# A two-layer network on one core: smaller first loads, a bank of its own for 256 columns, another order of GLA's state matmuls, and weight rows at shifted offsets

## Chip, cores and metric

The kernel runs on one core of one Trainium2 chip. The metric is the device time of one execution in microseconds. TensorE (PE) multiplies, VectorE (DVE) and ScalarE (ACT) work on tiles beside it, GpSimd (POOL) and SyncE (SP) do little but start transfers.

## What is computed

256 tokens of width 1024 pass two blocks and a last norm, all in float32.

```python
def first_block(x, mem, ...):
    h = rms_norm(x, norm_mix); z = h @ w_in
    z_rnn, z_q, z_k, z_v, z_g, z_dec, z_mq, z_gate = split(z)
    out_a = rg_lru(causal_dwconv(z_rnn))
    out_b = rms_norm(chunked_gla(z_q, z_k, z_v, log_alpha)) * silu(z_g)
    mk, mv = split(rms_norm(mem, mem_norm) @ w_mem_kv)
    out_c = softmax(z_mq @ mk.T) @ mv
    merged = sum(sigmoid(z_gate) * (branches @ w_branch))
    x = x + merged @ w_out
    gate_h, val_h = split(causal_dwconv(rms_norm(x) @ w_up))
    x = x + (gelu(gate_h) * val_h) @ w_down
    return rms_norm(x, final_norm)

# chunked_gla, per chunk of 64 tokens and per head:
    state = d_n[..., None] * state + einsum("bhjd,bhjv->bhdv", k_n, v_n)
```

The second block has attention with 6 heads, an SSD scan and a pooling mixer beside each other, then a SwiGLU FFN of width 2816 and the final norm, whose result is the output (256 x 1024).

## The kernel before

**Weights.** The kernel streams all weights once, in chunks of mostly 1024 x 256 (1 MB). A chunk is loaded by one DMA on SP's queue into one of three `raw` tiles and treated in two halves of four k rows (a k row: 128 partitions by 256 columns). Each half is split in two numbers, `wh` by a copy to the matmul's reduced type on ACT (L156) and `wl`, the rest, by a subtraction on DVE (L157); `emit_half` (L169 on) does both, three halves ahead of use (`AHEAD`), into five buffers each. The activations are kept split in the same way.

**Matmuls.** `mm3` (L202 to 205) makes one product from three matmuls: high by high, high by low, low by high. `chunk_T` holds the weights stationary and moves the 256 tokens, `chunk_tok` holds 128 tokens and moves 256 weight columns; both collect in one PSUM bank from the pool `psp`, of four, while everything else uses the four banks of `aup` (`aux`). `PLACE` puts both halves of the chunks up3, xbc3 and gu6 at an offset of 28 and 30 elements in their tiles; all other halves begin at 0.

**Order.** The chunks run in the order of `wplan`: memory keys and values (memk, memv), mq, zrnn, qk, the two gates of the recurrence, v, g, then for each of three branches four gate chunks alternating with four branch chunks (gate2_0, br2_0, ... gate0_0, br0_0, ... gate1_0, ...), wout, the first FFN (up and dn), the second block's input chunks (vz, qk2, xbc, pool), wo2, and the second FFN (gu and dn2_). Smaller pieces of work, as attention or GLA, are generators in two `lanes`; `step()` advances each by one `yield` between two chunks, and a tile scheduler fixes the order on each engine.

**GLA's state.** `gla_state` (L707 to 732) makes, for chunks 0, 1 and 2 of 64 tokens, k transposed times v for four heads. Chunk n stands on partitions 64 (n mod 2) on. Per chunk four matmuls of 64 rows (L720) fill two banks; ACT copies chunk 0, DVE adds the decayed state before for the others; then it yields. `gla_out` follows in the lane.

**Start.** The first two chunks, memk0 and memk1, are interleaved and come in pieces of two k rows: 128x512 of `memT` (the memory, transposed), then 128x512 of each chunk, four times, all on SP's queue; 16 columns of parameters (`par`, among them the norm gain that scales `memT`) come on ACT's queue. ACT scales and rounds memT (L159), DVE makes the rest (L160). Thirteen matmuls of ones (L258) run ahead of the first product. Sums of squares of memT are made with ACT (L282), DVE and two matmuls (L297).

**Second FFN and final norm.** `accs_tok` starts four banks with x3 transposed, two per tile of 128 tokens, of 512 columns each; `down_tok` adds every dn2_ chunk to them and `last_tok` the last ones, tile 0 first. Then, for each tile, ACT squares both banks (L1337) with a sum over columns, DVE adds the two sums (L1341, L1342), ACT takes the root (L1343), and four DVE instructions make the reciprocal and one Newton step (L1344 to 1347). For tile 1, the product of the first 512 columns with the gain `nfb` is made early, ACT scales it (L1354) and starts its DMA; DVE scales the other 512 in two pieces (L1331), each with a DMA on SP (L1360).

Of the kernel before, what the change touches and what calls it, by code (L numbers as in the profile page):

```python
# [9 lines left out]
F32 = mybir.dt.float32  # L10
# [63 lines left out]
for _n in ("up3", "xbc3", "gu6"):  # L74
    PLACE[_n, 0] = 28
    PLACE[_n, 1] = 30

# [38 lines left out]
def build(ctx: ExitStack, tc: tile.TileContext, ins: dict, out: bass.AP):  # L116
# [52 lines left out]
    def emit_half(parts=1, between=None):  # L169
# [12 lines left out]
        m = n // 2  # L182
        e = PLACE.get((name, i), 0)
# [47 lines left out]
    def chunk_tok(name, x, nk=KT, wide=False, k_outer=False):  # L231
# [3 lines left out]
        for i in range(2):  # L235
# [3 lines left out]
            if k_outer:  # L239
                od.sort(key=lambda q: q[1])  # L240
# [11 lines left out]
    par = cp.tile([P, NPAR], F32, name="par")  # L252
    nc.scalar.dma_start(par[:, :16], ins["par"][:, :16])
# [3 lines left out]
    for _ in range(13):  # L257
        pe.matmul(wps, ones, ones, start=True, stop=True)  # L258
    memr = slot("R1", [P, KT, S])
# [3 lines left out]
    def pv(name, i=0, n=1, rows=P):  # L263
        o, c = POFF[name]
        return par[:rows, o + i:o + i + n]
# [77 lines left out]
    def mem_part(i):  # L343
        nc.sync.dma_start(memr[:, 2 * i:2 * i + 2, :], ins["memT"][:, 2 * i:2 * i + 2, :])
        for k in (2 * i, 2 * i + 1):
            split(mh[:, k, :], ml[:, k, :], memr[:, k, :], pv("g_mem", k))


    first = ("memk0", "memk1")
    fps = [bank(), bank()]  # L350
    fw = {}
    for q in range(4):
        mem_part(q)
        for n, name in enumerate(first):
            if q == 0:
                raws[name] = wrp.tile([P, WMAX], F32, tag="raw", name=uid("raw"))
# [3 lines left out]
            o = WOFF[name][0]  # L360
            cr = slice(512 * q, 512 * q + 512)
            c = slice(512 * (q % 2), 512 * (q % 2) + 512)
            nc.sync.dma_start(raws[name][:, cr],
                              W[o:o + P * 2048].rearrange("(p n) -> p n", p=P)[:, cr])
            split(fw[n][0][:, c], fw[n][1][:, c], raws[name][:, cr])
            for k in range(2):
                for mo in range(2):
                    w0 = c.start + k * 256 + mo * P
                    kk = 2 * q + k
                    mm3(fps[n][:, mo, :], fw[n][0][:, w0:w0 + P], fw[n][1][:, w0:w0 + P],  # L370
                        mh[:, kk, :], ml[:, kk, :], kk == 0 and mo == 0, kk == KT - 1, skip=True)
# [13 lines left out]
    nc.sync.dma_start(par[:, 16:], ins["par"][:, 16:])  # L385
# [321 lines left out]
    def gla_state():  # L707
# [6 lines left out]
        for n in range(3):  # L714
            r = slice(64 * (n % 2), 64 * (n % 2) + 64)
            for hp in range(2):
                ps = aux([P, 2, DV])
                for i in range(2):
                    hd = 2 * hp + i
                    pe.matmul(ps[:DK, i, :], kt[r, n // 2, hd * DK:(hd + 1) * DK],  # L720
                              gv[r, n // 2, hd * DV:(hd + 1) * DV], start=True, stop=True)
                if n == 0:
                    act.activation(sts[0][:, hp * 384:(hp + 1) * 384],
                                   ps[:DK].rearrange("p a b -> p (a b)"), AF.Copy)
                else:
# [591 lines left out]
    def last_tok(ws, phs, accs):  # L1317
        act.activation(warm, last_u[0][:, 0, 0:1], AF.Sqrt, scale=0.0, bias=ones[:, 0:1])
        for t in range(2):
            c = slice(t * P, (t + 1) * P)  # L1320
            for n in range(2):
                q = slice(n * 512, (n + 1) * 512)
                for k, ((wh, wl), (ph, pl)) in enumerate(zip(ws, phs)):
                    mm3(accs[2 * t + n], ph[:, c], pl[:, c], wh[:, 0, q], wl[:, 0, q],
# [5 lines left out]
    def scaled(dst, acc, r, nf):  # L1330
        dve.scalar_tensor_tensor(dst, acc, r, nf, op0=ALU.mult, op1=ALU.mult)  # L1331

    for t in range(2):
        ssq = small([P, 2])
        o = [t2(), t2()]
        for n in range(2):
            act.activation(t2(), accs[2 * t + n], AF.Square, accum_out=ssq[:, n:n + 1])  # L1337
            if t == 1 and n == 0:
                dve.tensor_tensor(o[0], accs[2], nfb[:, 0:512], op=ALU.mult)
        v, r, q = small([P, 1]), small([P, 1]), small([P, 1])  # L1340
        dve.tensor_scalar(v, ssq[:, 0:1], 1.0 / D, EPS, op0=ALU.mult, op1=ALU.add)  # L1341
        dve.scalar_tensor_tensor(v, ssq[:, 1:2], 1.0 / D, v, op0=ALU.mult, op1=ALU.add)  # L1342
        act.activation(r, v, AF.Sqrt)  # L1343
        dve.reciprocal(r, r)  # L1344
        dve.tensor_tensor(q, r, r, op=ALU.mult)
        dve.scalar_tensor_tensor(q, q, -0.5, v, op0=ALU.mult, op1=ALU.mult)
        dve.scalar_tensor_tensor(r, q, 1.5, r, op0=ALU.add, op1=ALU.mult)
        rows = slice(t * P, (t + 1) * P)
        if t == 0:
            for n in range(2):  # L1350
                scaled(o[n], accs[n], r, nfb[:, n * 512:(n + 1) * 512])
                nc.sync.dma_start(out[rows, n * 512:(n + 1) * 512], o[n])
        else:
# [141 lines left out]
```

## Time and profile before

| | |
|---|---|
| runs | 796.61, 797.58, 798.03 us; median 797.58 us |
| profiled execution | 797.59 us |
| its span | 795.8 us |
| PE busy | 785.1 us (99%), 6460 records |
| DVE busy | 598.6 us (75%) |
| ACT busy | 481.8 us (61%) |
| DMA | 144.03 MB, mean 181 GB/s |
| granted TensorE clock, mean | 0.998 |

The span is what the profiler sees of the program; the profiled execution took 1.8 us more than it. Times in rows are counted from the span's start. A row of a timeline has the start, the duration of the instruction or the group (x count), the engine, the line, the operation with output and inputs, and in brackets the idle time ahead of it and what ended it. Matmuls overlap, so the starts of two neighbours tell their spacing, not their durations.

### The profile page before, as it was taken

How to read it: one execution, taken by the hardware profiler on the slowest of the kernel's cores; microseconds unless marked ns; L12 is line 12 of the kernel's file. 1: busy time of each engine (PE TensorE's matmuls, PEld its weight loads, DVE VectorE, ACT ScalarE, POOL GpSimd, SP SyncE). 2: the span in 40 equal slices, each digit the busy share in tenths (PEclk: the TensorE clock that was granted, in tenths of full speed). 3: DMA queues.
4: the chain of work that ended last, by engine and by line, in shares of the span. 5: the costliest groups of instructions: out<-in, count | busy, mean ns of one | idle time of the engine just before them, and what ended most of it. 6: DMA issues, size and time to landing. Idle time of an engine off the chain costs nothing.

```text
span 795.8 us, 15612 instructions
## 1 busy us (share of the span) xinstructions
PE 785.1 (99%) x6460; PEld 760.9 (96%) x6460; DVE 598.6 (75%) x980; ACT 481.8 (61%) x770; POOL 10.2 (1%) x23
## 2 busy tenths in 40 slices
PE   8999999999999999999999999999999999999996
PEld 8999989999889999999999999999899999999995
DVE  6988757965667777898778887899898756656663
ACT  6845679964345555666556565768976544444443
POOL 0000110000000000000000000000000000000000
PEclk9999999999999999999999999999999999999999
DMA  8864544364445665366555555263174544555521
GB/s 281 305 229 152 175 133 176 114 231 140 144 142 201 203 213 204 110 243 228 171 203 207 173 204 198 103 257 113 49 268 157 215 181 167 203 200 180 205 106 53
DMA packets 23526, 144.03 MB, mean 181 GB/s; under 512 B 2896, under 2 KB 3424, under 8 KB 8480
## 3 DMA queue, kind: packets, MB, share of 16 engines
q1 hardware_dynamic: 22464, 140.98, 49.9%
q0 software_dynamic: 704, 1.80, 0.6%
q8 instruction: 50, 0.82, 0.4%
q10 hardware_dynamic: 288, 0.27, 0.1%
q14 instruction: 20, 0.16, 0.1%
HBM read 141.20 MB, written 1.05 MB: 179 GB/s over the span
## 4 chain that ended last, share of the span: by engine, by line
PE 91%; DVE 4%; ACT 3%; issue 1%; DMA 1%; DVEq 0%; SPq 0%; ACTq 0%
PE ps L203 23%; PE ps L204 22%; PE ps L205 22%; PE aux L203 6%; PE aux L205 6%; PE aux L204 5%; DVE wl L157 2%; PE aux L521 1%; PE ps L220 1%; PE ps L227 1%; PE ps L218 1%; DMA raw<-w 1%; ACT wh L156 1%; PE aux L720 1%; ACT L1154 0%
## 5 line engine op out<-in xcount | busy, mean ns | idle before, releaser
L157 DVE TENSOR_TENSOR wl<-raw,wh 128x1024 fp32r<-128x1024 f32 (+4 forms) x276 | 322.1, 1172 | 119.5 <-ACT wh L156 117.7
L156 ACT ACTIVATE wh<-raw 128x1024 fp32r<-128x1024 f32 (+4 forms) x276 | 277.9, 1015 | 207.2 <-PE ps L204 159.6
L203 PE MATMUL ps<-H,wh 128*128 128x256 f32 x1320 | 368.2, 279 | 1.2 <-ACT wh L156 1.2
L205 PE MATMUL ps<-H,wl 128*128 128x256 f32 x1320 | 366.3, 278 | 0.2 <-DVE wl L157 0.2
L204 PE MATMUL ps<-H,wh 128*128 128x256 f32 x1320 | 366.3, 278 | 0.0
L203 PEld LDWEIGHTS ps<-H,wh 128*128 128x128 f32 x1320 | 248.0, 188 | 3.5 <-issue 1.8
L204 PEld LDWEIGHTS ps<-H,wh 128*128 128x128 f32 x1320 | 248.7, 188 | 0.3
L205 PEld LDWEIGHTS ps<-H,wl 128*128 128x128 f32 x1320 | 248.1, 188 | 0.4 <-DVE wl L157 0.4
L203 PE MATMUL ps<-wh,H 128*128 128x256 f32 (+2 forms) x192 | 54.6, 285 | 0.0
L204 PE MATMUL ps<-wl,H 128*128 128x256 f32 (+2 forms) x192 | 54.0, 281 | 0.3 <-DVE wl L157 0.3
L205 PE MATMUL ps<-wh,H 128*128 128x256 f32 (+2 forms) x192 | 54.1, 282 | 0.0
L205 PE MATMUL aux<-S,wl 128*128 128x256 f32 x192 | 53.1, 277 | 0.0
L204 PE MATMUL aux<-S,wh 128*128 128x256 f32 x192 | 53.1, 276 | 0.0
L203 PE MATMUL aux<-S,wh 128*128 128x256 f32 x192 | 53.1, 276 | 0.0
L156 ACT ACTIVATE S<-t 128x256 fp32r<-128x256 f32 x46 | 19.0, 415 | 50.3 <-DVE t L921 26.5
L543 DVE SCALAR_TENSOR_TENSOR t<-t,par,t 128x255 f32<-128x255 f32 (+1 forms) x96 | 40.1, 478 | 0.1
L204 PEld LDWEIGHTS ps<-wl,H 128*128 128x128 f32 x192 | 36.1, 188 | 0.5 <-DVE wl L157 0.5
L203 PEld LDWEIGHTS ps<-wh,H 128*128 128x128 f32 x192 | 36.1, 188 | 0.4 <-issue 0.4
L205 PEld LDWEIGHTS ps<-wh,H 128*128 128x128 f32 x192 | 36.1, 188 | 0.0
L205 PEld LDWEIGHTS aux<-S,wl 128*128 128x128 f32 x192 | 36.1, 188 | 0.0
L203 PEld LDWEIGHTS aux<-S,wh 128*128 128x128 f32 x192 | 36.1, 188 | 0.0
L204 PEld LDWEIGHTS aux<-S,wh 128*128 128x128 f32 x192 | 36.1, 188 | 0.0
(327 smaller groups left out, 1070.8 us busy)
## 6 DMA issues: line engine op xcount, KB each, us to landing
raw<-w SPq DMA_DIRECT2D x115, 1024.0 KB, 4.8
raw<-w SPq DMA_DIRECT2D x12, 768.0 KB, 4.3
raw<-w SPq DMA_DIRECT2D x12, 256.0 KB, 5.3
raw<-w SPq DMA_DIRECT2D x2, 896.0 KB, 4.5
raw<-w SPq DMA_DIRECT2D x1, 1088.0 KB, 6.2
raw<-w SPq DMA_DIRECT2D x1, 1048.0 KB, 4.8
R<-memT SPq DMA_DIRECT2D x4, 256.0 KB, 5.5
R<-xT SPq DMA_DIRECT2D x2, 512.0 KB, 8.8
```

The source lines that it names most:

```text
L156: act.activation(dst_h, src, AF.Copy)
L157: dve.tensor_tensor(dst_l, src, dst_h.bitcast(F32), op=ALU.subtract)
L203: pe.matmul(o, lh, rh, start=start, stop=False, skip_group_check=skip)
L204: pe.matmul(o, lh, rl, start=False, stop=False, skip_group_check=skip)
L205: pe.matmul(o, ll, rh, start=False, stop=stop, skip_group_check=skip)
L218: pe.matmul(ps[:, m, :], wh[:, k, c], x[0][:, kk, :], start=kk == 0 and m == 0, stop=False, skip_group_check=True)
L220: pe.matmul(ps[:, m, :], wl[:, k, c], x[0][:, kk, :], start=False, stop=False, skip_group_check=True)
L227: pe.matmul(ps[:, m, :], wh[:, k, m * P:(m + 1) * P], x[1][:, kk, :], start=False, stop=kk == nk - 1, skip_group_check=True)
L521: pe.matmul(ps[r0:r1, :], mv[:, mt, hd * DV + d0:hd * DV + d0 + r1 - r0], pts[hd][:, mt, :], start=mt == 0, stop=mt == 1, skip_group_check ...
L543: dve.scalar_tensor_tensor(dst[:, s:], src[:, :S - s], w(width - 1 - s), dst[:, s:], op0=ALU.mult, op1=ALU.add)
L720: pe.matmul(ps[:DK, i, :], kt[r, n // 2, hd * DK:(hd + 1) * DK], gv[r, n // 2, hd * DV:(hd + 1) * DV], start=True, stop=True)
```

## The change

- **Shifted rows.** A table `LEAD` names 14 chunks. In the first half of each, the first k row (or the first two) lies at an offset of 28 and 30 (or 4 and 2) modulo 32 elements of its tile, the rest at 0 modulo 32; `Rows` hands out the rows. The half is split in two pieces, so with two instructions on ACT and two on DVE. Entries that end in `True` run the first half with k outermost. `PLACE` gets gu3.
- **First loads.** The 16 parameter columns come in front of memT in the same tensor, so that the first piece is 128x272 on SP; the first two k rows of memk0 come as two pieces of 128x256 on ACT's queue; k row by k row is split for memk0. Ten matmuls of ones for thirteen.
- **GLA's state.** Chunks 0 and 1 take turns matmul by matmul, into four banks, and there are two yields in place of three.
- **Second FFN.** The last 512 columns of token tile 1 lie in two banks, of which one is taken from the pool of four that the chunks rotate through; in `down_tok` the runs of 256 go ahead of those of 512.
- **Final norm.** Another form of the root's correction, with doubled gains; for tile 1 all products are made part by part; one DVE instruction and one DMA for the second 512 columns.

The diff, cut:

```diff
-for _n in ("up3", "xbc3", "gu6"):
+for _n in ("up3", "xbc3", "gu6", "gu3"):
     PLACE[_n, 0] = 28
     PLACE[_n, 1] = 30
+LEAD = {
+    "mq1": (28, 30, True),
+    "qk0": (28, 30, True),
+    "gate2_0": (28, 30, True),
+    "gate0_1": (28, 30, True),
+    "gate0_3": (28, 30, True),
+    "memv0": (4, 2, True),
+    "v2": (28, 30, False),
+    "zrnn2": (28, 30, False),
+    "gate2_2": (28, 30, False),
+    "gu2": (28, 30, False),
+    "gate2_3": (28, False),
+    "gate0_0": (30, False),
+    "gate2_1": (4, 2, True),
+    "pool": (4, 2, False),
+}
+class Rows:
+    def __init__(self, t, b, n, lead):
+        self.t, self.b, self.n = t, b, n
+        self.off, o = [], 0
+        for k in range(n):
+            r = lead[k] if k < len(lead) else 0
+            o += (r - o) % 32
+            self.off.append(o)
+            o += b
+    def __getitem__(self, i):
+        _, k, c = i
+        a, e, _ = c.indices(self.b)
+        return self.t[:, self.off[k] + a:self.off[k] + e]
+    def parts(self):
+        b, n, m = self.b, self.n, self.lead
+        d = self.off[m - 1] - self.off[0] if m == 2 else b
+        head = self.t[:, self.off[0]:self.off[0] + m * d].rearrange("p (a b) -> p a b", a=m)[:, :, :b]
+        rest = self.t[:, self.off[m]:self.off[m] + (n - m) * b].rearrange("p (a b) -> p a b", a=n - m)
+        return (head, slice(0, m * b), m), (rest, slice(m * b, n * b), n - m)
...
+        if i == 0 and name in LEAD:
+            hs, ls = (Rows(w, b, a // 2, LEAD[name][:-1]) for w in (wh, wl))
+            for (h, c, r), (l, _, _) in zip(hs.parts(), ls.parts()):
+                split(h, l, raw[:, c].rearrange("p (a b) -> p a b", a=r))
+            loaded[name, i] = (hs, ls)
+            return
...
-            if k_outer:
+            if k_outer or i == 0 and LEAD.get(name, (False,))[-1]:
                 od.sort(key=lambda q: q[1])
...
+    nc.sync.dma_start(memall[:, :272], ins["memT"][:, :272])
+    for k in range(2):
+        first_w(nc.scalar, "memk0", slice(256 * k, 256 * k + 256))
+    nc.sync.dma_start(memr[:, 1, :], ins["memT"][:, 272:528])
+    first_w(nc.sync, "memk1", slice(0, 512))
...
+                if q == 0 and n == 0:
+                    c = slice(256 * k, 256 * k + 256)
+                    split(mh[:, kk, :], ml[:, kk, :], memr[:, kk, :], pv("g_mem", kk))
+                    split(fw[n][0][:, c], fw[n][1][:, c], raws[name][:, c])
...
-        for n in range(3):
-            r = slice(64 * (n % 2), 64 * (n % 2) + 64)
+        for ns in ((0, 1), (2,)):
             for hp in range(2):
-                ps = aux([P, 2, DV])
+                pss = [aux([P, 2, DV]) for _ in ns]
                 for i in range(2):
                     hd = 2 * hp + i
+                    for n, ps in zip(ns, pss):
+                        r = slice(64 * (n % 2), 64 * (n % 2) + 64)
...
+        accs = [aux([P, 512]) for _ in range(4)] + [bank([P, 512])]
...
+    RUNS = (((0, 0, 512), (1, 512, 512)), ((2, 0, 512), (3, 512, 256), (4, 768, 256)))
...
-                for n in range(2):
-                    q = slice(n * 512, (n + 1) * 512)
-                    mm3(accs[2 * t + n], ph[0][:, k, c], ph[1][:, k, c], wh[:, 0, q], wl[:, 0, q],
+                for a, q0, nq in sorted(RUNS[t], key=lambda r: r[2]):
+                    q = slice(q0, q0 + nq)
+                    mm3(accs[a][:, :nq], ph[0][:, k, c], ph[1][:, k, c], wh[:, 0, q], wl[:, 0, q],
...
+    act.activation(nfb, nfb, AF.Copy, scale=2.0)
...
+        for i, (a, q0, nq) in enumerate(parts):
+            act.activation(t2()[:, :nq], a[:, :nq], AF.Square, accum_out=ssq[:, i:i + 1])
+            if early:
+                q = q0 % 512
+                dve.tensor_tensor(o[q0 // 512][:, q:q + nq], a[:, :nq], nfb[:, q0:q0 + nq], op=ALU.mult)
...
+        act.activation(root, ssq[:, n - 1:], AF.Sqrt, scale=1.0 / D, bias=v[:, n - 2:n - 1])
+        dve.scalar_tensor_tensor(v[:, n - 1:], ssq[:, n - 1:], 1.0 / D, v[:, n - 2:n - 1],
+                                 op0=ALU.mult, op1=ALU.add)
+        dve.reciprocal(u, root)
+        dve.scalar_tensor_tensor(u, v[:, n - 1:], u, root, op0=ALU.mult, op1=ALU.add)
+        dve.reciprocal(u, u)
...
```

On ACT, at the start of the program, the kernel before has these rows (H is memT scaled and rounded, R is memT as loaded, t holds squares):

```order
L253 DMA par<-par 128x16
L255 ACT_TABLE_LOAD
L255 ACTIVATE warm<-ones 128x1
L159 ACTIVATE H_3_105<-R_1_102,par 128x256 x2
L156 ACTIVATE wh_115<-raw_114 128x512
L282 ACTIVATE t_22_277<-R_1_102 128x512
L156 ACTIVATE wh_133<-raw_132 128x512
L159 ACTIVATE H_3_105<-R_1_102,par 128x256 x2
```

and the changed one these:

```order
L315 DMA raw_86<-w 128x256 x2
L323 ACT_TABLE_LOAD
L323 ACTIVATE warm<-ones 128x1
L206 ACTIVATE H_5_108<-R_1_85 128x256
L203 ACTIVATE wh_112<-raw_86 128x256
L206 ACTIVATE H_5_108<-R_1_85 128x256
L203 ACTIVATE wh_112<-raw_86 128x256
L203 ACTIVATE wh_134<-raw_87 128x512
L206 ACTIVATE H_5_108<-R_1_85 128x256 x2
```

The parameter load is gone from ACT's queue and two weight loads stand there; one k row of memT and 256 columns of memk0 are split at a time, and the first square has moved behind them.

On TensorE, in the lane of GLA, the first group of state matmuls of the kernel before stands between a branch chunk and a gate chunk (V holds k transposed, S holds v, aux are PSUM banks):

```order
L205 MATMUL ps_2175<-M_159_1286,wl_2115 128x256
L720 MATMUL aux_2226<-V_204_1543,S_271_2087 96x192 x2
L720 MATMUL aux_2230<-V_204_1543,S_271_2087 96x192 x2
L203 MATMUL ps_2234<-H_39_325,wh_2144 128x256
```

and in the changed kernel, at the same place:

```order
L258 MATMUL ps_2191<-M_159_1294,wl_2129 128x256
L792 MATMUL aux_2242<-V_204_1551,S_271_2101 96x192
L792 MATMUL aux_2243<-V_204_1551,S_271_2101 96x192
L792 MATMUL aux_2242<-V_204_1551,S_271_2101 96x192
L792 MATMUL aux_2243<-V_204_1551,S_271_2101 96x192
L792 MATMUL aux_2251<-V_204_1551,S_271_2101 96x192
L792 MATMUL aux_2252<-V_204_1551,S_271_2101 96x192
L792 MATMUL aux_2251<-V_204_1551,S_271_2101 96x192
L792 MATMUL aux_2252<-V_204_1551,S_271_2101 96x192
L256 MATMUL ps_2260<-H_39_327,wh_2158 128x256
```

The group now holds eight matmuls for chunks 0 and 1 in turn, in four banks; a second group of four, for chunk 2, stands where the second of three stood, and what follows in the lane stands one place earlier.

On DVE, at the end of the program, for token tile 1, before (aux are the banks of the result, GQ the gain, sm columns of one number):

```order
L1339 TENSOR_TENSOR t_1202_9471<-aux_8024,GQ_7605 128x512
L1341 TENSOR_SCALAR sm_9478<-sm_9470 128x1
L1342 SCALAR_TENSOR_TENSOR sm_9478<-sm_9470,sm_9478 128x1
L1344 RECIPROCAL sm_9479<-sm_9479 128x1
L1345 TENSOR_TENSOR sm_9480<-sm_9479 128x1
L1346 SCALAR_TENSOR_TENSOR sm_9480<-sm_9480,sm_9478 128x1
L1347 SCALAR_TENSOR_TENSOR sm_9479<-sm_9480,sm_9479 128x1
L1331 SCALAR_TENSOR_TENSOR t_1203_9472<-aux_8025,sm_9479,GQ_7605 128x256 x2
```

and in the changed kernel:

```order
L1422 TENSOR_TENSOR t_1206_9569<-aux_8052,GQ_7631 128x512
L1425 TENSOR_SCALAR sm_9566<-sm_9565 128x1
L1422 TENSOR_TENSOR t_1207_9570<-aux_8053,GQ_7631 128x256
L1427 SCALAR_TENSOR_TENSOR sm_9566<-sm_9565,sm_9566 128x1
L1422 TENSOR_TENSOR t_1207_9570<-ps_8054,GQ_7631 128x256
L1430 SCALAR_TENSOR_TENSOR sm_9566<-sm_9565,sm_9566 128x1
L1432 RECIPROCAL sm_9567<-sm_9568 128x1
L1433 SCALAR_TENSOR_TENSOR sm_9567<-sm_9566,sm_9567,sm_9568 128x1
L1434 RECIPROCAL sm_9567<-sm_9567 128x1
L1444 TENSOR_SCALAR t_1207_9570<-t_1207_9570,sm_9567 128x512
```

The products with the gain stand ahead of the root's steps, in three parts; one step fewer stands between the last sum and the scaling, and the scaling of the second 512 columns is one instruction.

## Rows read from the trace of the kernel before

**Rows 1.** The page, sections 1, 4 and 5 (busy us, mean ns, idle us).
```profile
PE 785.1 (99%) x6460; PEld 760.9 (96%) x6460; DVE 598.6 (75%) x980; ACT 481.8 (61%) x770; POOL 10.2 (1%) x23
...
PE 91%; DVE 4%; ACT 3%; issue 1%; DMA 1%; DVEq 0%; SPq 0%; ACTq 0%
...
L156 ACT ACTIVATE wh<-raw 128x1024 fp32r<-128x1024 f32 (+4 forms) x276 | 277.9, 1015 | 207.2 <-PE ps L204 159.6
L203 PE MATMUL ps<-H,wh 128*128 128x256 f32 x1320 | 368.2, 279 | 1.2 <-ACT wh L156 1.2
```

**Rows 2.** Waits of PE: line, releaser, us in total, times, longest us.
```profile
PE aux L1086 <- ACT S L1154: 1.4, 1, 1.4
```

**Rows 3.** Windows: stretch, length, busy and count of each engine, PEclk, DMA share, GB/s.
```profile
28.40:42.30 13.90, 13.90 (x121) 13.90 (x120) 13.90 (x23) 11.93 (x22) 0.00 (x0) 1.00 0.69 249
133.90:153.50 19.60, 19.60 (x168) 19.60 (x168) 18.45 (x14) 18.03 (x22) 0.96 (x1) 1.00 0.27 95
250.90:315.90 65.00, 65.00 (x576) 65.00 (x575) 49.59 (x59) 36.41 (x46) 0.00 (x0) 1.00 0.57 199
325.20:330.80 5.60, 5.60 (x50) 5.60 (x49) 4.59 (x8) 3.96 (x8) 0.00 (x0) 1.00 0.56 187
331.20:504.80 173.60, 173.60 (x1534) 173.60 (x1533) 145.77 (x234) 107.87 (x164) 0.00 (x0) 1.00 0.54 189
619.70:638.90 19.20, 19.20 (x165) 19.20 (x164) 14.56 (x23) 10.77 (x18) 0.00 (x0) 1.00 0.49 181
```

**Rows 4.** Timeline of PE at the first group of GLA state matmuls.
```profile
175.29 1.54 PE L720 MATMUL aux<-V,S 64*96 64x192 f32 x8
176.76 0.38 PE L203 MATMUL ps<-H,wh 128*128 128x256 f32 x1
```

**Rows 5.** Timeline of PE in the second layer's attention: two heads, and one head.
```profile
536.83 0.50 PE L976 MATMUL aux<-M 64*128 64x128 f32 x4
...
537.70 0.43 PE L327 MATMUL aux<-cst,sm 128*128 128x128 f32 x2
...
544.63 0.38 PE L976 MATMUL aux<-M 64*128 64x128 f32 x2
...
545.22 0.48 PE L976 MATMUL aux<-M 64*128 64x128 f32 x2
```

**Rows 6.** Timeline of ACT at the start.
```profile
5.26 0.91 ACT L159 ACTIVATE H<-R,par 128x256 fp32r<-128x256 f32 x2 [2.59 <-DMA par<-par]
6.20 0.63 ACT L156 ACTIVATE wh<-raw 128x512 fp32r<-128x512 f32 x1
```

**Rows 7.** Timeline of DVE at the start.
```profile
5.81 0.88 DVE L160 SCALAR_TENSOR_TENSOR H<-R,par,H 128x256 fp32r<-128x256 f32 x2 [4.80 <-ACT H L159]
6.87 0.69 DVE L157 TENSOR_TENSOR wl<-raw,wh 128x512 fp32r<-128x512 f32 x1 [0.18 <-ACT wh L156]
7.91 0.69 DVE L157 TENSOR_TENSOR wl<-raw,wh 128x512 fp32r<-128x512 f32 x1 [0.35 <-ACT wh L156]
```

**Rows 8.** Windows of the first two chunks, columns as in rows 3.
```profile
7.00:12.00 5.00, 4.78 (x39) 4.57 (x40) 4.65 (x10) 5.00 (x12) 0.00 (x0) 1.00 1.05 387
12.00:19.00 7.00, 6.95 (x60) 6.74 (x58) 7.00 (x13) 5.05 (x11) 0.00 (x0) 1.00 0.86 300
```

**Rows 9.** Timeline of PE in the last microsecond of matmuls.
```profile
788.38 0.39 PE L205 MATMUL aux<-wh,S 128*128 128x512 f32 x1
788.61 0.39 PE L203 MATMUL aux<-wh,S 128*128 128x512 f32 x1
```

**Rows 10.** Timeline of ACT behind the last matmul.
```profile
789.56 0.60 ACT L1337 ACTIVATE t<-aux 128x512 f32<-128x512 f32 x1 [2.06 <-PE aux L205]
```

**Rows 11.** Timeline of DVE behind the last matmul.
```profile
791.29 0.16 DVE L1347 SCALAR_TENSOR_TENSOR sm<-sm,sm 128x1 f32<-128x1 f32 x1
791.49 0.88 DVE L1331 SCALAR_TENSOR_TENSOR t<-aux,sm,GQ 128x256 f32<-128x256 f32 x2
```

**Rows 12.** Timeline of SP's queue behind the last matmul.
```profile
792.00 0.81 SPq L1360 DMA_DIRECT2D out_dram<-t  x2
```

More of the change, by code (lines that the diff above doesn't have):

```diff
@@ L238, in chunk_tok @@
             od = [(t, k) for t in range(2) for k in range(nk // 2)]
-            if k_outer:
+            if k_outer or i == 0 and LEAD.get(name, (False,))[-1]:
                 od.sort(key=lambda q: q[1])
@@ L251, in build, with first_w @@
     dve.memset(ones, 1.0)
-    par = cp.tile([P, NPAR], F32, name="par")
-    nc.scalar.dma_start(par[:, :16], ins["par"][:, :16])
+    par = cp.tile([P, NPAR - 16], F32, name="par")
+    memall = slot("R1", [P, 16 + KT * S])
+    memr = memall[:, 16:].rearrange("p (k s) -> p k s", k=KT)
+    first = ("memk0", "memk1")
+    for n in first:
+        raws[n] = wrp.tile([P, WMAX], F32, tag="raw", name=uid("raw"))
+    def first_w(queue, name, c):
+        o = WOFF[name][0]
+        queue.dma_start(raws[name][:, c], W[o:o + P * 2048].rearrange("(p n) -> p n", p=P)[:, c])
+    nc.sync.dma_start(memall[:, :272], ins["memT"][:, :272])
[3 more added lines that the diff above has]
+    first_w(nc.sync, "memk1", slice(0, 512))
     warm = cp.tile([P, 1], F32, name="warm")
@@ L264, in pv @@
         o, c = POFF[name]
-        return par[:rows, o + i:o + i + n]
+        if o < 16:
+            return memall[:rows, o + i:o + i + n]
+        return par[:rows, o - 16 + i:o - 16 + i + n]
     def cv(name):
@@ L341, in build @@
     m = (mh, ml)
[L343 to L349, printed above, removed]
     fps = [bank(), bank()]
@@ L352, in build @@
     for q in range(4):
-        mem_part(q)
+        ks = (2 * q, 2 * q + 1)
+        if q > 0:
+            nc.sync.dma_start(memr[:, ks[0]:ks[1] + 1, :],
+                              ins["memT"][:, 16 + 512 * q:16 + 512 * q + 512].rearrange("p (a b) -> p a b", a=2))
+            for k in ks:
+                split(mh[:, k, :], ml[:, k, :], memr[:, k, :], pv("g_mem", k))
         for n, name in enumerate(first):
-            if q == 0:
-                raws[name] = wrp.tile([P, WMAX], F32, tag="raw", name=uid("raw"))
             if q % 2 == 0:
@@ L1292, in accs_tok @@
                     k = 4 * n + i
-                    pe.matmul(accs[2 * t + n][:, i * P:(i + 1) * P], x3[:, k, t * P:(t + 1) * P], ident,
-                              start=i == 0, stop=False, is_transpose=True, skip_group_check=True)
+                    a, f = accs[2 * t + n], i == 0
+                    if t == 1 and n == 1 and i > 1:
+                        a, i, f = accs[4], i - 2, i == 2
+                    pe.matmul(a[:, i * P:(i + 1) * P], x3[:, k, t * P:(t + 1) * P], ident,
+                              start=f, stop=False, is_transpose=True, skip_group_check=True)
         return accs
+    RUNS = (((0, 0, 512), (1, 512, 512)), ((2, 0, 512), (3, 512, 256), (4, 768, 256)))
     def down_tok(name, ph, accs, first, last):
@@ L1327, in build @@
     accs = ffn(("gu", "dn2_"), NF2, (x3h, x3l), s3, "nA", ffn2_body, down_tok, last_tok, accs_tok)
-    def scaled(dst, acc, r, nf):
-        dve.scalar_tensor_tensor(dst, acc, r, nf, op0=ALU.mult, op1=ALU.mult)
-    for t in range(2):
[L1334 to L1353, printed above, removed]
-            act.activation(o[0], o[0], AF.Copy, scale=r)
-            nc.scalar.dma_start(out[rows, 0:512], o[0])
-            for i in range(2):
-                c = slice(256 * i, 256 * i + 256)
-                cc = slice(512 + 256 * i, 768 + 256 * i)
-                scaled(o[1][:, c], accs[3][:, c], r, nfb[:, cc])
-                nc.sync.dma_start(out[rows, cc], o[1][:, c])
@@ L1363, in tcol @@
+    for t in range(2):
+        final([(accs[a], q0, nq) for a, q0, nq in RUNS[t]], slice(t * P, (t + 1) * P), t == 1)
 def tcol(v):
```

65 lines of the change are left out of this document (43 added, 22 removed).

## Prediction

> **What bounds the kernel now.** I read the page's first and fourth sections before anything else: TensorE is busy for 785.1 of 795.8 us and the chain that ended last lies on it for 91% of the span [rows 1]. So a cut counts only if it takes time out of TensorE's own stream, or out of the few places where TensorE waits or has nothing left to do. The waits come second: they are few and short, the longest being 1.4 us for a value that ACT makes in the second layer [rows 2]. The ends of the span come third: the stage of the first two chunks at the start, and the norm behind the last matmul. Last I asked whether TensorE's stream itself runs evenly, since 1% of it is worth more than all waits. The windows answer that. In each the granted clock is 1.00 [rows 3], and a matmul of 128x256 lasts 0.28 us [rows 1], so that (length + 0.28) / count is the spacing of their starts. From gate1_0 to up1, and from up4 to dn11, it is 65.28/576 = 113.3 ns and 173.88/1534 = 113.4 ns; in the value chunks of the memory branch 14.18/121 = 117.2, from v2 to g2 19.88/168 = 118.3 and in gu2 to gu5 19.48/165 = 118.1 ns [rows 3]; gate2_2, gate0_0 and the stretch from gate0_2 to br0_3 are three more of that loose kind. There are two spacings, tight and loose, 4.4 ns apart, at one clock, and a stretch keeps its spacing. The one shifted chunk whose window I show, up3, runs at 5.88/50 = 117.6 and what follows it is tight [rows 3]; the two other chunks that the kernel before shifts have tight spacing behind them as well. That is three of three, but in all three both halves are shifted whole.
>
> The sum below is made against the profiled execution: 797.59 us, of which 795.8 is span. The median of the runs is 797.58, so no correction is needed.
>
> **Shifted rows.** Each listed chunk gets one or two k rows of its first half at another offset, 6 to 12 matmuls of 48 (the gate chunks run k outermost there, so that the shifted rows come first). If a shifted row does what the three shifted chunks seem to do, the loose stretches behind it turn tight. Those that have a list entry at their head, in matmuls: memv0 to memv2 144, v2 to g2 192, gate2_2 with its branch chunk 84, gate0_0 with its branch chunk 84, gate0_1 to br0_3 (two entries; 168 matmuls of it, from gate0_2 on, are loose now) 168, gu2 to gu5 192. With 12 matmuls of each still loose, and all 48 of gu3, which is now shifted whole, that is 132 + 180 + 72 + 78 + 144 + 132 = 738 matmuls by 4.4 ns = 3.2 us less. Eight entries stand in stretches that are tight already; there they cost at most 8 x 12 x 4.4 ns = 0.4 us. memv0 is the first shifted chunk whose weights are the moving operand, and offsets 4 and 2 stand nowhere in the kernel before; I count half of its 0.58 us. Net: -3.2 + 0.4 + 0.3 = **-2.5 us**; from -3.2 to +0.4 (no effect behind them, shifted rows loose).
>
> The half's split becomes two instructions on ACT and on DVE: 2 x 0.63 us for 512 elements [rows 6] against 1.02 for 1024 [rows 1], so +0.24 us on either engine, 14 times. ACT is busy 61% and DVE 75%, with splits running up to three halves ahead, and this hides it everywhere but at the pool chunk. There ACT is the late one and TensorE already waits 1.4 us for it [rows 2]; the second piece stands ahead of what is waited for: **+0.25 us** (0 to +0.35).
>
> **State matmuls.** Before, chunk by chunk, a group of 8 records takes 176.76 - 175.29 = 1.47 us [rows 4], three times, 4.4 us on the path. In the changed order chunks 0 and 1, which sit on rows 0 to 63 and 64 to 127, alternate. That two row halves run beside each other the attention of the second layer shows: two heads on the two halves take 537.70 - 536.83 = 0.87 us for the work for which one head alone takes 545.22 - 544.63 = 0.59 [rows 5], so a pair costs 0.74 of two single heads. In the best case 2 x 1.47 become 1.47, by that ratio 2.17. The state records are 1.47 / 8 = 0.18 us apart, more than the 0.12 of a matmul of 256 columns on all rows, so it is the row halves that stand idle, not the columns; I take the best case less little: **-1.4 us** (0 to -1.7, with the changeover of one group that goes). The rest of this branch moves one step earlier; its consumers get more time, not less, and I price that at nothing. Its cover is the gate chunk that stands between; if it failed, gla_out would wait for DVE's state updates, at 0.44 us each by the nearest row [rows 11].
>
> **Start.** H's first piece waits until 5.26 for the small parameter load on ACT's queue; both k rows are split (0.91), then 512 weight columns (0.63) [rows 6]. The parameters now ride with the first piece of memT, and k row 0 and 256 columns suffice for the first matmul, 0.46 + 0.42 for 0.91 + 0.63, some 0.6 us less. That is not yet the gain, because DVE ends this stage: it is busy 4.65 of 5.0 us from 7 to 12 and 7.00 of 7.00 from 12 to 19 [rows 8]. What counts is how much earlier DVE begins and how many gaps it loses. It begins at 5.81, behind H's first row, and has gaps of 0.18 and 0.35 ahead of the first two weight splits [rows 7]. The piece it waits for has 136 KB now and not 256; 120 KB are 0.3 us at the 387 GB/s that the transfers reach [rows 8]. The gaps, 0.5 us, go since half a weight split is ready after the first row, and one more split in two costs DVE 0.15. **-0.7 us** (-0.2 to -1.5, the upper end if the first piece lands well ahead because the 64 byte rows of the parameter load are gone). The two loads that ACT issues lie ahead of its table load, in time in which it waits.
>
> In the stretch from 7 to 12 us the transfers, of 256 KB, move 387 GB/s [rows 8], so pieces of that size do not starve the start; none of 128 KB is in the trace. The Trainium skill, "DMA: Bandwidth & Descriptors", section Bandwidth, advises to batch to 1 MiB and more, and gives 0.95 us for 64 KB against 6.15 us for 1 MB; by that the two 128 KB pieces would cost some tenths more than one of 256 KB, an estimate from that page, and the start would give nearer -0.4. No run here shows it yet.
>
> **Second FFN's down projection.** The last 512 columns of token tile 1 become two runs of 256, 22 k rows by 3 matmuls: 66 pairs. A 512 wide matmul is followed by the next after 0.23 us [rows 9]; a pair takes 2 x 113.4 to 2 x 118 = 227 to 236 ns. That is -0.2 to +0.4 us, and a changed sequence may put the gu chunks behind it at the other spacing, so I take **+0.1** (-0.4 to +0.8). One bank less rotates for gu; a chunk takes over 5 us and its eviction ends well inside the next, so three are enough.
>
> **Tail.** The chain behind the last matmul is Square over 512 columns (0.60) [rows 10], read-out, a DVE step, Sqrt, four DVE steps 0.20 apart, the scaling (2 x 0.44) [rows 11] and the output transfers, of which SP issues two in 0.81 us [rows 12]. After: Square over 256, about -0.15; the DVE step ahead of Sqrt goes, -0.2; three steps for four, -0.2; one transfer of 256 KB issued for two, less its longer flight, -0.2. New is DVE's product of the last 256 columns, 0.44 us, which reads the bank that Square reads and stands ahead of the remaining DVE steps: +0.3. Sum **-0.45** (-0.1 to -0.8). Doubling the gains costs ACT one 128x1024 instruction, near 1.02 us, where ACT has slack; without that slack TensorE would wait about as long.
>
> **Sum:** -2.5 + 0.25 - 1.4 - 0.7 + 0.1 - 0.45 = -4.7, so 797.59 - 4.7 = **792.9 us**.
>
> **The rivals.** *The spacing does not follow the row's offset.* Then the shift gives nothing and costs nothing, and 797.59 - 2.2 = 795.4. For it: the three cases are shifted whole, and one of the listed chunks may turn the spacing for a reason that I cannot see. Against it: the loose stretches have matmuls of as many columns as the tight ones, at the same clock [rows 3]. The Trainium skill, "TensorE: Matmul & The Clock Gate", section Back-to-back issue gap, has the isolated gap as columns over 2.4 GHz plus 2.5 ns, nothing else; by it, 109 ns everywhere, there would be no second spacing to win. The trace disagrees, with 113.3 and 118 [rows 3].
>
> *Rows on the two halves do not run beside each other with this shape, and the start is held by landings.* Then 1.4 and 0.4 us are lost: 794.7.
>
> *The entry at gate0_3 does the opposite.* The transposes of GLA's output, which stand between br0_3 and gate1_0 now, move ahead of gate0_3, so that nothing but chunks lies between its entry and the end of up1. If its aligned rows keep the loose spacing, the 576 matmuls behind it [rows 3] lose 4.4 ns each, 2.5 us: 795.4. For it: that stretch is tight without an entry now.
>
> *All entries lock the loose spacing*, the case on the other side. An offset row would then end a tight stretch until the next other kind of matmul. Behind entries in stretches that are tight now stand 216 + 96 + 4 x 84 + 500 + 48 = 1196 matmuls, 5.3 us; the shift costs 5.3 where I take -2.5, and the time is 797.59 - 2.2 + 5.3 = 800.7. It decides against the change from about 500 locked matmuls on, where the other gains of 2.2 us are eaten. Against it speak the three shifted chunks, for it only that the half rows are new.
>
> **How the numbers follow.** Forecast 0.62; no effect of offsets 0.13; no overlap and late landings 0.10; gate0_3 0.08; all loose 0.07. The forecast's own bounds, not all at one end, are 791.2 to 794.7; to hold 8 in 10 I stretch to the cases at 795.4 with half a microsecond beside them: 791.2 to 796.2. A measurement here tells about 0.2%, 1.6 us, from no change: faster is below 796.0, slower above 799.2. The forecast, the second rival and most of the first and third are faster, 0.85; the rest of these two within, 0.08; all loose, 0.07.
>
> **What would show it.** Windows over memv1 to memv2, g0 to g2, gate2_2, gate0_0, gate0_2 to br0_3 and gu4 to gu5 near 113.4 ns; the window from gate1_0 to up1 still at 113.3; state groups two in number, 1.5 us each; DVE's first instruction near 5.3 us and the stage's last wait at about 18.5; from the last matmul's end to the last output issue 0.4 us less. I am wrong first if spacing is set by something that the offsets of two rows do not reach, and then if a tight stretch behind an entry turns loose.

## The result and the profile after

The changed kernel takes 801.69 us (801.35 to 801.77, four runs) against 797.62 for the kernel before: a ratio of 1.0052, interval 1.0035 to 1.0069. It is slower by 4 us where 4.7 us less were forecast, and outside the stated range. The profiled execution took 801.77 us, its span is 800.0.

The page of the changed kernel, sections 1 and 4, against [rows 1]: TensorE is still the bound, with 5.7 us more of busy time.

```profile
span 800.0 us, 15765 instructions
...
PE 790.8 (99%) x6520; PEld 770.1 (96%) x6520; DVE 599.9 (75%) x995; ACT 483.7 (60%) x788; POOL 10.2 (1%) x23
...
PE 94%; ACT 3%; DVE 1%; DMA 1%; issue 1%; SPq 0%; ACTq 0%
```

The waits of TensorE in the changed kernel, as in [rows 2]: the one at the pool chunk is shorter by 0.5, and one behind the first chunks (L366) is new. No wait explains 4 us.

```profile
PE aux L1159 <- ACT S L1227: 0.9, 1, 0.9
PE aux L366 <- DVE t L361: 0.8, 1, 0.8
```

The windows do, with the columns of [rows 3]: memv, mq1 to zrnn1, v2 to g2, gate1_0 to up1, most of up4 to dn11, gu4 to gu5.

```profile
27.60:41.50 13.90, 13.90 (x121) 13.90 (x120) 13.90 (x24) 13.13 (x27) 0.00 (x0) 1.00 0.61 239
51.00:70.30 19.30, 19.30 (x166) 19.30 (x165) 14.55 (x21) 10.88 (x16) 0.00 (x0) 1.00 0.50 178
134.40:153.90 19.50, 19.50 (x168) 19.50 (x168) 18.34 (x15) 18.11 (x23) 0.96 (x1) 1.00 0.27 96
249.50:314.50 65.00, 65.00 (x576) 65.00 (x576) 48.51 (x58) 36.40 (x46) 0.00 (x0) 1.00 0.59 207
330.00:503.40 173.40, 173.40 (x1475) 173.40 (x1474) 141.69 (x224) 103.06 (x156) 0.00 (x0) 1.00 0.54 189
634.00:643.60 9.60, 9.60 (x87) 9.60 (x86) 7.66 (x13) 5.72 (x10) 0.00 (x0) 1.00 0.63 218
```

By (length + 0.28) / count, the matmuls of up4 to dn11 start 173.68/1475 = 117.7 ns apart where it was 113.4 [rows 3]: over all of them, some 1530, 6.8 us more. mq1 to zrnn1 is 19.58/166 = 118.0; before, the same matmuls were tight:

```profile
51.50:70.30 18.80, 18.80 (x168) 18.80 (x168) 14.12 (x19) 10.72 (x14) 0.00 (x0) 1.00 0.53 182
```

that is 19.08/168 = 113.6. memv and v2 to g2 stayed loose, 117.2 and 117.7, and gu4 to gu5 turned tight, 113.6. The clock is 1.00 throughout. Summed over the records of all chunk matmuls of 256 columns from memv to gu5, the time beyond 113.3 ns each rose by 7.6 us: 6.8 in up4 to dn11, 0.4 in xbc0 and qk2_2, 0.4 net in the rest. All that is not spacing gave 7.6 - 4.2 = 3.4 us back.

What is odd about it: up4 to dn11 is not behind any new entry. It is behind up3, which the change does not touch. Instructions, tiles, banks and addresses of up2, up3 and up4 are the same in both kernels. The timeline of TensorE at the head of up3, before and then after:

```profile
324.96 0.38 PE L327 MATMUL aux<-cst,sm 128*128 128x128 f32 x2
325.10 0.37 PE L203 MATMUL ps<-H,wh 128*128 128x256 f32 x1
325.30 0.28 PE L204 MATMUL ps<-H,wh 128*128 128x256 f32 x1
325.42 0.28 PE L205 MATMUL ps<-H,wl 128*128 128x256 f32 x1
```

```profile
323.53 0.38 PE L396 MATMUL aux<-cst,sm 128*128 128x128 f32 x2
323.67 0.37 PE L256 MATMUL ps<-H,wh 128*128 128x256 f32 x1
323.87 0.29 PE L257 MATMUL ps<-H,wh 128*128 128x256 f32 x1
324.00 0.28 PE L258 MATMUL ps<-H,wl 128*128 128x256 f32 x1
```

The second and the third matmul of up3 are 0.12 us apart before and 0.13 after (120 and 126 ns in the records). From there on the two run through up3 in different rhythms, each 118 ns on the mean, and leave it in different spacings. Right ahead of up3 stand two transposes (L327, now L396) that read the identity from the tile of constants, cst. It is the one tile read by TensorE that lies elsewhere: packing 16 parameter columns in front of memT made the parameter tile 64 bytes shorter, and cst slid from address 88128 to 88064 (bytes within a partition, from the program). The tile of memT slid with it, but TensorE never reads that one.

### The profile page after: what moved, and what is told of

Its sections match the earlier page's. It is cut to its first block, busy times and chain, and to the rows that moved or that the text cites. A ratio compares the mean times of both kernels' runs of the same rounds, so it can differ in the third digit from the quotient of the medians.

```text
span 800.0 us, 15765 instructions
## 1 busy us (share of the span) xinstructions
PE 790.8 (99%) x6520; PEld 770.1 (96%) x6520; DVE 599.9 (75%) x995; ACT 483.7 (60%) x788; POOL 10.2 (1%) x23
## 4 chain that ended last, share of the span: by engine, by line
PE 94%; ACT 3%; DVE 1%; DMA 1%; issue 1%; SPq 0%; ACTq 0%
PE ps L256 24%; PE ps L257 24%; PE ps L258 24%; PE aux L256 5%; PE aux L257 5%; PE aux L258 5%; ACT wh L203 1%; PE aux L591 1%; PE ps L280 1%; PE ps L271 1%; PE ps L273 1%; DMA R<-memT 1%; PE aux L821 0%; PE aux L827 0%; DVE wl L204 0%
## 5 line engine op out<-in xcount | busy, mean ns | idle before, releaser
L257 PE MATMUL aux<-S,wh 128*128 128x256 f32 x192 | 54.0, 281 | 0.0
L256 PE MATMUL aux<-S,wh 128*128 128x256 f32 x192 | 54.0, 281 | 0.0
```

Of the source, the lines that this page charges most:

```text
L256: pe.matmul(o, lh, rh, start=start, stop=False, skip_group_check=skip)
L257: pe.matmul(o, lh, rl, start=False, stop=False, skip_group_check=skip)
```

## The experiments

The theories: A, the address of the identity sets the phase in which up3 is entered, and by that the spacing in which it is left (a phase is here the pattern of spacings in which a chunk's matmuls follow one another; no view shows what lies behind it); B, the entries further ahead carry over.

**Constants moved in the kernel before.**

```diff
     ones = cp.tile([P, P], F32, name="ones")
+    cst = cp.tile([P, NCST], F32, name="cst")
     par = cp.tile([P, NPAR], F32, name="par")
...
-    cst = cp.tile([P, NCST], F32, name="cst")
```

> The kernel before, with the tile of constants (cst, which holds the identity that the transposes read) allocated ahead of the parameters: it moves from address 88128 (64 modulo 128) to 86656 (0 modulo 128), every streamed tile stays where it was. In the changed kernel cst also moved, by 64 bytes, and there the unchanged shifted chunks up3 and xbc3, which stand right behind transposes that read cst, are followed by matmuls 117.8 ns apart instead of 113.3. Theory A, the address of what the transposes read sets the phase in which a shifted chunk begins: up4 to dn11 turn loose, about +6.4 us, xbc0 to qk2_2 too, +0.4; mq0 and qk2 may turn tight, -0.4: some 804 us. Theory B, the shifted rows in chunks further ahead or the other timing of the changed kernel carry over to up3: nothing changes, 797.6 us.

Measured: 797.32 us, ratio 0.9997 (0.9988 to 1.0007). A failed here: up4 to dn11 stayed tight. The move only turned mq0 tight and shuffled the first chunks. So "0 modulo 128" is not what matters; 86656 is 128 modulo 256 and 88064 is 0.

**Constants moved in the changed kernel.**

```diff
-    ones = cp.tile([P, P], F32, name="ones")
+    ones = cp.tile([P, 120], F32, name="ones")
...
+    cst = cp.tile([P, NCST], F32, name="cst")
-    warm = cp.tile([P, 1], F32, name="warm")
+    warm = cp.tile([P, 16], F32, name="warm")[:, 0:1]
...
```

> The changed kernel with the 32 bytes behind ones and the constants rearranged so that cst lies at 88000 (64 modulo 128, as in the kernel before) and all else where it was; the warm-up matmuls have 120 columns for 128. Theory A: up4 to dn11 and xbc0 to qk2_2 turn tight again, -6.5 and -0.4 us, rga to v0 perhaps too, -0.45: about 794.5 us, faster than the kernel before. Theory B: 801.7 us, nothing changes.

Measured: 793.81 us, ratio to the kernel before 0.9957 (0.9942 to 0.9971): 7.9 us less than the changed kernel, by where a few small tiles lie. Its windows over mq1 to zrnn1 and over up4 to dn10:

```profile
50.80:69.50 18.70, 18.70 (x167) 18.70 (x166) 14.49 (x22) 10.98 (x16) 0.00 (x0) 1.00 0.51 181
...
329.00:495.00 166.00, 166.00 (x1467) 166.00 (x1466) 140.51 (x223) 103.26 (x154) 0.00 (x0) 1.00 0.55 195
```

18.98/167 = 113.7 and 166.28/1467 = 113.3 ns. By the traces, 6.8 of it are up4 to dn11, 0.4 xbc0 and qk2_2, and 0.7 mq1 to zrnn1. The last is not settled by the address: at the same 88000 that stretch is loose in the four other runs below.

**Without the entries, and the entries alone.** In the first, `LEAD` is empty and gu3 not in `PLACE`; in the second, the kernel before has `LEAD`, `Rows` and gu3.

> The changed kernel without its 14 entries of shifted rows and without gu3's shift; all other parts are kept, cst stays 64 bytes lower. Theory A: up4 to dn11 stay loose, since the constants are where the changed kernel has them; the time moves by what the entries themselves do, between -0.5 and +2 us: 801 to 804. Theory B (entries carry over): up4 to dn11 turn tight, 801.7 - 6.5 plus the entries' own gains of some 1 us: about 796.

> The kernel before with the 14 entries of shifted rows and gu3's shift alone; start, state matmuls, second FFN and norm are the old ones, cst stays at its old address. Theory A: up4 to dn11 stay tight, and the entries give what the prediction priced, -2.5 us, or less where an entry fails: 795 to 798. Theory B: up4 to dn11 turn loose, about +6.4: 802 to 804.

Measured: 801.20 us without the entries, up4 to dn11 loose; 798.14 with the entries alone (ratio 1.0010, 1.0000 to 1.0019), up4 to dn11 tight. Their windows over that stretch, in this order:

```profile
329.00:502.00 173.00, 173.00 (x1471) 173.00 (x1470) 141.30 (x223) 102.68 (x155) 0.00 (x0) 1.00 0.53 189
```

```profile
332.50:504.00 171.50, 171.50 (x1515) 171.50 (x1515) 144.27 (x230) 106.17 (x160) 0.00 (x0) 1.00 0.54 191
```

173.28/1471 = 117.8 and 171.78/1515 = 113.4. B falls: the entries neither make nor cure it. And by themselves they gave nothing where the prediction had them give 2.5: 0.5 us more, with an interval that begins at no change.

**The same address in the kernel before, and a neighbour in the changed one.**

```diff
-    ones = cp.tile([P, P], F32, name="ones")
+    ones = cp.tile([P, 120], F32, name="ones")
     par = cp.tile([P, NPAR], F32, name="par")
+    cst = cp.tile([P, NCST], F32, name="cst")
...
```

> The kernel before with the constants at 88064, where the changed kernel has them (the tile of ones is 120 columns wide and the parameters come first; all streamed tiles stay). At 86656 they did nothing to up4 to dn11, so this tells whether the address itself is the cause. Address theory: up3's second matmul starts 126 ns after its first and not 120, up4 to dn11 turn loose, +6.8 us, xbc0 to qk2_2 +0.4: about 804.8 us. If something else of the changed kernel is needed too: 797.6 us.

> The changed kernel with the constants at 87808, again a multiple of 256, but not of 512 (ones 64 columns wide, the warm-up matmuls too). If every multiple of 256 is a bad place: 801.7 us, up4 to dn11 loose. If only the larger multiple, 512 or 1024, is bad, or that one address: up4 to dn11 tight, about 794 us.

Measured: 804.80 us, ratio 1.0094 (1.0079 to 1.0109); and 801.19 at 87808. That the first is the number forecast is in part luck: the kernel before took 796.72 us beside it, so it is 8.1 more where 7.2 were forecast, and in the trace mq1 to zrnn1 is loose too, 0.8 us that neither theory had. The timeline of TensorE at up3 in the kernel before with cst at 88064, and its window:

```profile
325.61 0.38 PE L327 MATMUL aux<-cst,sm 128*128 128x128 f32 x2
325.75 0.37 PE L203 MATMUL ps<-H,wh 128*128 128x256 f32 x1
325.95 0.29 PE L204 MATMUL ps<-H,wh 128*128 128x256 f32 x1
326.08 0.28 PE L205 MATMUL ps<-H,wl 128*128 128x256 f32 x1
```

```profile
332.00:504.00 172.00, 172.00 (x1463) 172.00 (x1462) 141.04 (x222) 102.52 (x154) 0.00 (x0) 1.00 0.53 189
```

0.13 us again (what the expectation calls up3's first and second matmul are its second and third), and 172.28/1463 = 117.8 ns. The tile of ones, the address of the parameters and the columns of the warm-up matmuls are here as in the run at 88000, where up4 to dn11 were tight. So the address alone does it, in the old kernel too, and both multiples of 256 that were tried are bad (344 and 343 times 256), while 64, 128 and 192 modulo 256 are good.

**Which reader of the constants.** The two transposes ahead of up3 get a copy of the identity; cst stays at 88064.

```diff
+        if names[0] == "up":
+            idt = slot("S5", [P, P])
+            act.activation(idt, ident, AF.Copy)
...
-                st["r"] = widen(rt, rtag)
+                st["r"] = widen(rt, rtag, idt)
...
```

> The changed kernel, constants at 88064, but the two transposes that stand right ahead of up3 read a copy of the identity at 208448 (64 modulo 256); the copy costs ACT some 0.3 us. If what these transposes read sets the phase in which up3 begins: its second matmul starts 120 ns after the first and not 126, up4 to dn11 turn tight, -6.8 us: about 794.9, while xbc0 to qk2_2 stay loose. If the other readers of cst further ahead matter: 801.7 us.

Measured: 794.89 us, 6.8 less than the changed kernel. In the timeline the transposes now read S, and up3 starts as in the kernel before:

```profile
323.32 0.38 PE L396 MATMUL aux<-S,sm 128*128 128x128 f32 x2
323.46 0.37 PE L256 MATMUL ps<-H,wh 128*128 128x256 f32 x1
323.67 0.28 PE L257 MATMUL ps<-H,wh 128*128 128x256 f32 x1
323.79 0.28 PE L258 MATMUL ps<-H,wl 128*128 128x256 f32 x1
```

xbc0 and qk2_2, behind the other pair of transposes, stayed loose. What two matmuls of 128 columns read decides the spacing of some 1530 that follow. A copy at a bad address was not run.

**The other half of the phase.** Same bad address, up3 and xbc3 shifted by 30 and 28 for 28 and 30.

> The changed kernel, constants at its own bad address 88064, with the offsets of up3 and xbc3 swapped: 30 in the first half and 28 in the second. If the exit spacing follows from the phase in which the chunk is entered and from the offsets together, another pair of offsets may well leave in the tight spacing: then up4 to dn11 and perhaps xbc0 to qk2_2 are tight and the time is 794 to 795. If at this address no shift helps, 801.7.

Measured: 794.64 us. Windows over up4 to dn10 and over xbc0 and qk2_2:

```profile
329.90:495.00 165.10, 165.10 (x1459) 165.10 (x1459) 139.64 (x222) 103.08 (x154) 0.00 (x0) 1.00 0.55 195
...
524.40:535.30 10.90, 10.90 (x95) 10.90 (x94) 10.26 (x29) 7.36 (x10) 0.00 (x0) 1.00 0.59 210
```

165.38/1459 = 113.4 ns behind up3, but 11.18/95 = 117.7 behind xbc3: the swap helps at one of the two. The shift is not wrong as such; whether it leaves a chunk tight hangs on the address read just before, on the pair of offsets and on the chunk.

**What the entries are worth in the good layout.**

> The changed kernel with the constants at 88000, where it ran in 793.81 us, and without the 14 entries and gu3's shift: what the entries are worth in the good layout. By the prediction, 2.5 us more: 796.3. By the run of the entries alone on the kernel before, where they cost 0.5 us: 793.3.

> The changed kernel with the constants at 88000 and only four of the entries (gate0_1, gate0_3, gate2_2, gu2) and gu3's shift, those behind which the trace shows tight spacing where it was loose before. If each entry acts for itself, the loose rows of the entries left out go: 0.6 us less, 793.2. If what an entry does hangs on the phase that the entries ahead of it leave, some of the four fail: 793.8 or more.

> The run with the constants at 88000 and four entries (793.44 us), with the entries of mq1 and gate2_1 added, ahead of the two long stretches that are still loose there: mq1 to zrnn1 (0.86 us too long) and gate2_0 to br2_3. If each entry acts for itself: 0.7 us less at mq1 and some 0.3 at gate2_1, 792.4. If the entries ahead change how later groups are entered: one of the gains is given back behind it, 793 to 794.

Measured: 793.62 without entries, 793.44 with four, 793.43 with six, 793.81 with all 14. Against the kernel before, run beside each, the ratios are 0.9966, 0.9955, 0.9951 and 0.9957, each known to about 0.0015, so none can be told from another. Of the ten runs without entries two took 797.1 and 797.4, the others 793.1 to 794.0; the profile caught one of the two, with gate0_1 to up1 loose:

```profile
249.50:314.50 65.00, 65.00 (x555) 65.00 (x554) 47.35 (x57) 35.20 (x46) 0.00 (x0) 1.00 0.56 197
```

65.28/555 = 117.6 ns for the 113.3 of the kernel before. This is the third rival's stretch, loose where gate0_3 has no entry; no run with that entry showed it, but most of those kernels ran four to six times, too few to call it a protection. In the runs with four and six, gate0_1, gate0_3, gate2_2 and gu2 left their chunks tight. In the run with six gate2_1 did too, but mq1's entry did not turn mq1 to zrnn1 tight, though in the run with all 14 at the same address it was tight.

**The old state matmuls.** `gla_state` of the kernel before in the changed kernel with cst at 88000.

> The changed kernel with the constants at 88000 (793.81 us) and the state matmuls of the kernel before, chunk by chunk in three groups. If the turns of two row halves save what the trace of the changed kernel shows (16 records in the time of 8): 1.5 us more, 795.3. If that time is won back elsewhere: 793.8.

Measured: 796.57 us, 2.8 more, and not 1.5. The trace has the 1.5, three groups for two; the rest is spacing: mq1 to zrnn1 loose, 0.7, and gate0_2 to br0_3 loose as in the kernel before, 0.6 us. Their windows:

```profile
51.00:70.00 19.00, 19.00 (x164) 19.00 (x163) 14.52 (x21) 10.75 (x16) 0.00 (x0) 1.00 0.50 169
227.20:246.90 19.70, 19.70 (x169) 19.67 (x168) 13.05 (x25) 8.57 (x13) 0.00 (x0) 1.00 0.41 139
```

19.28/164 = 117.6 and 19.98/169 = 118.2 ns. The first stands 100 us ahead of the state matmuls, behind code that is the same in both, so they did not make it; that the start did, where TensorE waits for loads, is likely but was not tried. The second goes with the state matmuls: with the entries of gate0_1 and gate0_3 it is tight in all seven kernels with the new ones and loose in both with the old.

## Why the prediction was wrong, point by point

**Shifted rows, -2.5 us: the step that failed.** I took from three shifted chunks that a shifted row ends a loose stretch, and priced stretches by it. What the runs show is a phase: an address read just before, and the offsets, together set in which of two rhythms a chunk is left. Of the 14 entries, nine left their chunk tight in the changed kernel and five loose (memv0, mq1, v2, gate2_0, gate0_0). In the four changed kernels without the entries of v2 and gate0_0, v2 to g2 and gate0_0 are tight; in every kernel with them they are loose. Windows over v2 to g2 and gate0_0 to br0_0 in the run without entries (801.20 us):

```profile
132.10:151.80 19.70, 19.70 (x176) 19.70 (x175) 17.71 (x14) 18.95 (x23) 0.96 (x1) 1.00 0.30 102
201.50:210.40 8.90, 8.90 (x81) 8.90 (x80) 6.64 (x18) 3.63 (x6) 0.00 (x0) 1.00 0.29 88
```

19.98/176 = 113.5 and 9.18/81 = 113.3 ns. At mq1 and gate2_0 the stretch had been tight, but these turn loose in kernels without an entry there as well, mq1 in three and gate2_0 in four. In all the entries gave no gain: +0.5 us alone, at the edge of the noise, and nothing that can be told in the good layout. The three cases were three samples of one phase each, and I read them as a rule; two of them, up3 and xbc3, turned with the address.

**What was left out: the larger part of the miss.** The sum took every chunk outside the list at no change, without a reason. But +6.8 and +0.4 us came from behind up3 and xbc3, two chunks that the change leaves as they were, by way of a 64 byte shorter tile. I had the sizes of the tiles and did not compare the addresses. The last sentence of the prediction names such a case, a spacing set by something that the offsets do not reach, but no term or rival had a price for it. The time lies near the rival in which all entries lock the loose spacing (800.7), but that is not what happened: without any entry it is 801.20.

**State, -1.4 us: right.** Timeline of TensorE at the two groups of the changed kernel, against [rows 4]:

```profile
176.21 1.54 PE L792 MATMUL aux<-V,S 64*96 64x192 f32 x16
177.68 0.39 PE L256 MATMUL ps<-H,wh 128*128 128x256 f32 x1
...
187.52 1.54 PE L792 MATMUL aux<-V,S 64*96 64x192 f32 x8
188.98 0.38 PE L256 MATMUL ps<-H,wh 128*128 128x256 f32 x1
```

16 records end where 8 did; with one group of 1.47 us gone, the gain is 1.5 us. That the rest of the branch moves one step earlier was priced at nothing; by the run with the old state matmuls it is worth another 0.6 us, through the spacing of gate0_2 to br0_3.

**Start, -0.7 us: the size right (-0.55), the way wrong.** DVE does begin earlier, at 4.05 for 5.81 [rows 7], but then waits for memk1's weights, and ends the stage where it did: its last step of the sum of squares starts at 18.71, and at 18.72 before. Timelines of DVE, first the start, then that step, and of ACT at the first 512 columns of memk1:

```profile
4.05 0.48 DVE L207 SCALAR_TENSOR_TENSOR H<-R,H 128x256 fp32r<-128x256 f32 x1 [3.05 <-ACT H L206]
...
7.37 0.69 DVE L204 TENSOR_TENSOR wl<-raw,wh 128x512 fp32r<-128x512 f32 x1 [1.20 <-ACT wh L203]
...
18.71 0.42 DVE L361 TENSOR_TENSOR t<-t 128x256 f32<-128x256 f32 x1
```

```profile
6.71 0.63 ACT L203 ACTIVATE wh<-raw 128x512 fp32r<-128x512 f32 x1 [1.08 <-DMA raw<-w]
```

DVE's 1.20 us wait for them takes back what came earlier: ACT idles 1.08 us there for the load, so the transfers hold the start after all. By the trace the gain came through the order: five matmuls of memk2 run ahead of the wait for the sum now (L366, 0.8 us in the waits above), 5 x 0.113 = 0.57 us.

**Pool, +0.25 us: wrong sign, small.** The wait there went from 1.4 to 0.9 us. It goes with the entry: 0.7 to 1.0 us in all seven kernels with the entry of pool, 1.2 to 1.4 in the seven without it. Waits of TensorE in the run with the entries alone, then in the changed kernel without them:

```profile
PE aux L1139 <- ACT S L1207: 0.9, 1, 0.9
```

```profile
PE aux L1144 <- ACT S L1212: 1.4, 1, 1.4
```

So the second split does not delay the value that TensorE waits for; how it brings it forward is open.

**Down projection, +0.1:** -0.1 between gu6 and the last dn2_ chunk, within its bounds.

**Tail, -0.45 us: right.** Timelines of DVE and of ACT behind the last matmul, then of TensorE at its last matmul, before and after:

```profile
794.70 0.42 DVE L1422 TENSOR_TENSOR t<-ps,GQ 128x256 f32<-128x256 f32 x1 [0.93 <-ACT t L1419]
795.04 0.15 DVE L1430 SCALAR_TENSOR_TENSOR sm<-sm,sm 128x1 f32<-128x1 f32 x1
...
795.75 0.49 DVE L1444 TENSOR_SCALAR t<-t,sm 128x512 f32<-128x512 f32 x1
```

```profile
794.19 0.38 ACT L1419 ACTIVATE t<-ps 128x256 f32<-128x256 f32 x1 [0.95 <-PE ps L258]
...
794.70 0.29 ACT L1429 ACTIVATE sm<-sm,sm 128x1 f32<-128x1 f32 x1
795.75 0.72 ACT L1441 ACTIVATE t<-t,sm 128x512 f32<-128x512 f32 x1 [0.76 <-DVE sm L1434]
```

```profile
789.06 0.40 PE L205 MATMUL aux<-wh,S 128*128 128x512 f32 x1
```

```profile
793.82 0.28 PE L258 MATMUL ps<-wh,S 128*128 128x256 f32 x1
```

From the start of the last Square to that of the scaling it is 1.56 us for 1.93 [rows 10, 11]. From the end of the last matmul (793.82 + 0.28) to the end of the span it is 5.90 for 6.34 us before (789.06 + 0.40 to 795.8): -0.44. So 0.37 came up to the scaling, where the sum's terms give 0.25, and only 0.07 around it, where the output transfers were to give 0.2; the parts' errors cancel. DVE's product of the last 256 columns (0.42) is in front of the root's steps, as feared.

So the terms besides spacing, 0.55 + 1.5 + 0.5 + 0.1 + 0.44, sum to -3.1 us where -2.2 were forecast (0.3 of the 3.4 above I cannot assign), and the spacing to +7.6 where it was -2.5.

## What to carry to other kernels

Where a profile shows two rhythms of the same instruction at one clock, compare the addresses of every operand of the two kernels, not only the instructions: a tile that becomes 64 bytes shorter moves all that lie behind it. Price such an effect from as many entries as the change makes, at the places where it makes them, and hold a rival in which an untouched place flips. And give a change that moves memory a twin in which the memory is moved back, before its parts are judged: the same code at a better address took 793.8 us for 801.7, and 7.2 of these 7.9 us lie behind the two chunks that follow the moved tile's transposes.

## What the hardware showed that was not expected

- A stream of 128x256 matmuls held one of two spacings, 113.3 or 117.8 ns, at a granted clock of 1.00, for up to 1530 matmuls in a row; it changed across shifted chunks, waits or other kinds of matmul. The Trainium skill, "TensorE: Matmul & The Clock Gate", section Back-to-back issue gap, has columns over 2.4 GHz plus 2.5 ns, 109 for 256, for an isolated matmul, and says that in a stream of weight loads and matmuls both set the spacing, with values for 128 and 512 columns alone. These runs are such a stream, so the formula that the prediction held against them does not bind here, and they show two values for 256 columns.
- Which one it held behind a shifted chunk hung on the address that two 128-column transposes ahead of the chunk read: loose at 87808 and 88064, tight at 86656, 88000, 88128 and 208448. With the offsets swapped (30 and 28) it turned tight at 88064 as well behind up3, but not behind xbc3. What in the chip has this phase is open, and so is why the first chunks, where TensorE waits for loads, come out differently from run to run, in code that is the same.
- Matmuls of 64 rows on the two halves ran at twice the rate: 16 records in 1.47 us for 8.
